# Three gate-column buffers and three one-hot buffers instead of two and four, with smaller kept tiles, in a decoder step on one core

## The chip, the cores and the metric

One core of one Trainium2 chip runs the whole program. The metric is the device time of one execution in microseconds (us); the median of three runs is shown, and beside it one execution under the hardware profiler. Engines are named as the profile names them: PE (TensorE, matrix products), DVE (VectorE), ACT (ScalarE), POOL (GpSimd, here only the issuer of row gathers) and SP (SyncE, here only the issuer of the other DMA transfers). Each engine works through its own queue in order, so an instruction that waits holds everything behind it on that engine.

## The reference, cut to what matters

The reference is one decoder layer for 512 prompt tokens and 64 sample tokens (576 rows of width 1024). Attention and a gating unit come first and give x1. The part that the change touches is the retrieval of single-neuron experts behind it:

```
sc = einsum('thcd,hcnd->thcn', q, sub_keys)             # 8 heads, 2 halves, 128 keys
s_top, i_top = top_k(sc, 16);  best, pos = top_k(sums of the two halves, 16)
idx = i*128 + j of the 16 best pairs                    # 16384 experts
gate = softmax(best)
w = gate * gelu(expert_u[idx] . x);  out[t] = sum_k w_k * expert_v[idx_k]
x2 = x1 + out;   x3 = x2 + sigmoid(rmsnorm(x2) @ w_ple_gate) * (p @ w_ple)
```

## The kernel before

The 576 columns are cut in two kinds. The 64 sample tokens and 128 of the prompt tokens are done by *gathering*: POOL fetches each token's expert rows from HBM by index (L726), and DVE makes the dot products (L737) and later the weighted sums (L744). The other 384 prompt tokens are done *densely*: for all 128 blocks of 128 experts, stage 1 computes gelu(u x) for all 384 tokens, the result is multiplied by a gate matrix G which is zero except at the retrieved experts, and stage 2 multiplies by v.

Stage 1 for one block j (function `stage1`, L781) loads 512 KB of weights by SP (L75), splits them on ACT into a rounded part `w_hi` (L70) and on DVE into the rest `w_lo` (L71), issues 24 PE products of 384 columns (L86) and one ACT gelu (L795). Results stay in SBUF, or are spilled to `ad` and fetched back.

G is built between about 572 and 817 us of the span by `build_g` (L856), called for `tb` = 0 to 23, 16 tokens each. It has four groups of four tokens. A group is: DVE writes the one-hot rows and columns `hot` (L870); ACT (L876, four instructions) or DVE (L879) scales one half by the gate into `og`; PE makes 8 small f16 products (L887) into a PSUM bank; ACT copies the bank into the gate-column tile `gs` (L891). After four groups one DMA writes the 1 MB of `gs` to `gd` in DRAM (L894), in runs of 512 bytes. `hot` and `og` come from the pool `op` with `OPB` = 4 buffers each; `gs` comes from two single pools in turn (L860, L916), so the first copy of block tb waits until the DMA of block tb-2 has landed. The build of G shares PE, ACT and DVE with stage 1, with the last top-k work of retrieval (up to `tb` = 7) and with gathers.

The order on each engine is fixed when the kernel is built, from the order of the program and from priorities given by hand: the splits of weights are drawn forward (L78, offset 1000), the products and copies of G too (L884, offset `RUNP` = 400), and `after` (L94) places an instruction behind another without a semaphore. How many gathers are issued between two steps is a budget (`pay`, L769). How many stage-1 blocks stand between two calls of `build_g` is a goal by arithmetic (L929 to L934).

Behind the last block the pools of the build are closed (L946), and their place is used by stage 2 (L947 to L949): `wh`, `wl`, `x1c` and two tiles `gs` of 12 KB per partition that bring G back. To spare the first of these a round trip, the columns of the last block go through a small tile `g0` (L928, written at L893, read at L1055).

Small tiles that live long: `ones` (128 x 128, L104) for sums over partitions at L158, L185 and L576; `eps` (three columns, L101); `dots`, `idx` and `gate` of the two gathered tiles (L734, L711, L695), each with two buffers of full width.

Of the kernel before, what the change touches and what calls it, by code (L numbers as in the profile page):

```python
# [7 lines left out]
F32 = mybir.dt.float32  # L8
# [3 lines left out]
U32 = mybir.dt.uint32  # L12
# [6 lines left out]
P = 128  # L19
# [5 lines left out]
NJ = 128  # L25
TB = 16
JB = 8
# [8 lines left out]
S1_TOPK = (4, 9, 13)  # L36
TBK = 7
S1_END = 6
OPB = 4
G_LAG = 3  # L40
RUNP = 400
RING = 44
# [9 lines left out]
def tile_decoder_step(ctx: ExitStack, tc: tile.TileContext, a, o):  # L52
    nc = tc.nc
    V, A, T, G, S = nc.vector, nc.scalar, nc.tensor, nc.gpsimd, nc.sync

    def pool(stack, name, bufs, side="left", **kw):
        return stack.enter_context(tc.tile_pool(name=name, bufs=bufs, side=side, reuse_waits="tile", **kw))

    const = pool(ctx, "const", 1)
# [34 lines left out]
    def after(ins, earlier):  # L94
        tc.add_manual_dep(ins.ins, earlier.ins.name, mybir.DependencyInfo(
            mybir.DependencyClass.NoSync, mybir.DependencyReason.DATA), reason="pace")
# [1 line left out]
    def mm():  # L98
        return psM.tile([P, 512], F32, name="mm")

    eps = const.tile([P, 3], F32, name="eps")  # L101
    V.memset(eps[:, 0:1], EPS)
    V.memset(eps[:, 1:2], 64.0 * EPS)
    ones = const.tile([P, P], F32, name="ones")  # L104
    V.memset(ones, 1.0)
    x1d = dr.tile([KC, P, NB], F32, name="x1d")
    x1r = dr.tile([NB // P, P, D], F32, name="x1r")
    pld = dr.tile([NT, D], F32, name="pld")
# [7 lines left out]
    c4 = pool(c4s, "c4", 7, "right")  # L116
    e1 = pool(e1s, "e1", 2, "right")
    e2 = pool(e2s, "e2", 2, "right")

    def f4(dt=F32):  # L120
        return c4.tile([P, 4, NT], dt, name="c4")
# [11 lines left out]
    def bank(tag):  # L133
        return psB.tile([P, 512], F32, name=tag)
# [19 lines left out]
    def rstd_cols(tot, rs):  # L154
        ps = bank("sc")
        for c0, r in TILES:
            for p0 in range(0, P, r):
                T.matmul(ps[p0:p0 + r, c0 // P:c0 // P + 1], lhsT=tot[:, c0:c0 + r], rhs=ones[:, 0:1],  # L158
                         start=True, stop=True)
        A.activation(rs, ps[:, 0:5], AF.Sqrt, scale=1.0 / D, bias=eps[:, 0:1])  # L160
        V.reciprocal(rs, rs)
# [10 lines left out]
    tot, add = sumsq()  # L172
# [9 lines left out]
    with tc.high_priority(offset=500):  # L182
        for cols in HALVES:
            ps = bank("sc")[:, :cols.stop - cols.start]
# [289 lines left out]
    for i in range(24):  # L474
        if i < 8:
            t, g = (svT, suT)[i // 4], i % 4
# [36 lines left out]
    gp = pool(ctx, "gp", 2)  # L513
# [8 lines left out]
    tot, add = sumsq()  # L522
# [43 lines left out]
    tq = pool(tqs, "tq", 2)  # L566
    tks = ExitStack()
    tk = pool(tks, "tk", 1, "right")
    rn2 = tq.tile([P, NB], F32, name="rn2", bufs=1)

    def norm_row():
        ps = bank("pt")[:, :NB]
        for b in range(3):
            dg = tq.tile([P, P], F32, name="dg")
            A.activation(dg, ident, AF.Copy, scale=rs2[:, b + 1:b + 2])
            T.matmul(ps[:, b * P:(b + 1) * P], lhsT=ones, rhs=dg, start=True, stop=True)  # L576
        A.activation(rn2, ps, AF.Copy)

    def norm_x(k):
# [38 lines left out]
    def retrieve(ti, idx_out):  # L618
        nh = TOPK[ti][1]
        n = nh * 16  # L620
        s0, s1 = top[ti][:, 0, :nh], top[ti][:, 1, :nh]

        def new(name, shape, dt=BF16, pl=tk, **kw):
            t = pl.tile([P, 8] + list(shape), dt, name=name, **kw)
            return t[:, :nh]
# [66 lines left out]
        V.tensor_tensor(bb.rearrange("p h k -> p (h k)"), pos.rearrange("p h k -> p (h k)"), stv, op=ALU.subtract)  # L692
        bbp = spread(bb)
        e0 = lookup("e0", ge, d0[:, :, None, :].to_broadcast([P, nh, 16, 16]), False, 1)
        gt = new("gate", [16], F32, gp if idx_out else tk, bufs=2)  # L695
        V.tensor_tensor(gt, best, best[:, :, 0:1].to_broadcast([P, nh, 16]), op=ALU.subtract)
        b_ = TOPK[ti][0]
        A.activation(gt, gt, AF.Exp, scale=rs2[:, b_:b_ + 1])
# [9 lines left out]
        if not idx_out:  # L708
            found[ti] = e0, e1, gtf
            return  # L710
        idx = gp.tile([P, P], U32, name="idx")  # L711
        V.scalar_tensor_tensor(idx[:, :n], e1, 128.0, e0, op0=ALU.mult, op1=ALU.add)
        ixs.append(idx)
        gts.append(gtf)
# [16 lines left out]

    def gather_steps():
        for ti, ns in ((0, NS), (1, P)):
            dots = gp.tile([P, P], F32, name="dots")  # L734
            for s in range(ns):
                row_ = gather_row(a["peer_u"], ixs[ti][:, s:s + 1])
                V.scalar_tensor_tensor(row_, row_, 1.0, xrs[ti], op0=ALU.mult, op1=ALU.mult,  # L737
                                       accum_out=dots[:, s:s + 1])
                yield
            A.activation(dots[:, :ns], dots[:, :ns], AF.Gelu_apprx_tanh)  # L740
            V.tensor_tensor(dots[:, :ns], dots[:, :ns], gts[ti][:, :ns], op=ALU.mult)
            for s in range(ns):
                row_ = gather_row(a["peer_v"], ixs[ti][:, s:s + 1])
                V.scalar_tensor_tensor(accs[ti], row_, dots[:, s:s + 1], accs[ti], op0=ALU.mult, op1=ALU.add)  # L744
                yield
# [69 lines left out]
    held_x = [xp.tile([P, 6, NB], F32, name="x4") for _ in range(NXP // 6)]  # L815
# [40 lines left out]
    def build_g(tb):  # L856
        ti, t0 = divmod(tb * TB, P)
        ij, gpk = ewT[ti]
        gate = gpk.rearrange("p t h -> p (t h)").bitcast(F32)
        gs = gsp[(tb + 1) % 2].tile([P, NJ, TB], F32, name="gs")  # L860
        for t4 in range(0, TB, 4):
            pt = psB.tile([P, 512], F32, name=("sc", "pt")[t4 // 4 % 2])
            hot = op.tile([P, 2, 2, P, 2], F16, name="hot")
            og = op.tile([P, 4, P], F32, name="og")
            u0 = (t0 + t4) // 2

            def wide(x):
                return x.rearrange("p u f t -> p (u f) t")[:, :, None, :].to_broadcast([P, 4, P, 2])

            V.tensor_tensor(hot.rearrange("p u f j t -> p (u f) j t"), iota[:, None].to_broadcast([P, 4, P, 2]),  # L870
                            wide(ij[:, u0:u0 + 2]), op=ALU.is_equal)
            grp = tb * TB // 4 + t4 // 4
            c = t0 + t4
            if grp % 4 < 3 if tb < TBK else grp % 3 < 2:
                for t in range(4):
                    last = A.activation(og[:, t, :], hot[:, t // 2, 1, :, t % 2], AF.Copy,  # L876
                                        scale=gate[:, c + t:c + t + 1])
            else:
                last = V.tensor_tensor(og.rearrange("p (u t) j -> p u t j", t=2),  # L879
                                       hot[:, :, 1].rearrange("p u j t -> p u t j"),  # L880
                                       gate[:, c:c + 4].rearrange("p (u t) -> p u t", t=2)[:, :, :, None]
                                       .to_broadcast([P, 2, 2, P]), op=ALU.mult)
            right = og.rearrange("p t j -> p (t j)").bitcast(F16).rearrange("p (t j h) -> p t j h", t=4, h=2)
            with tc.high_priority(offset=RUNP):  # L884
                for t in range(4):
                    for h in range(2):
                        g_last[tb] = T.matmul(pt[:, t * P:(t + 1) * P], lhsT=hot[:, t // 2, 0, :, t % 2],  # L887
                                              rhs=right[:, t, :, 1 - h], start=h == 0, stop=h == 1)
                        if t == h == 0:
                            after(g_last[tb], last)  # L890
                A.activation(gs[:, :, t4:t4 + 4], pt.rearrange("p (t j) -> p j t", t=4), AF.Copy, scale=1.0 / GS)  # L891
        if tb == NB // TB - 1:
            A.activation(g0, gs[:, 0:JB, :], AF.Copy)  # L893
        S.dma_start(gd[:, :, tb].rearrange("c p j t -> p c (j t)"), gs.rearrange("p (c j) t -> p c (j t)", j=JB))  # L894
# [18 lines left out]
    gs_s = ExitStack()  # L913
    ep = pool(gs_s, "ep", 2)
    op = pool(gs_s, "op", OPB)
    gsp = [pool(gs_s, "gsp%d" % i, 1) for i in range(2)]  # L916
    phase[0] = 1
    rest_t = [retrieve(ti, False) for ti in (3, 4)]
    for tb in range(NB // TB):
        if tb == TBK:  # L920
            for i, r_ in enumerate(rest_t):
                for _ in r_:
                    pass
                make_ew(*found[5 - len(rest_t) + i])
            tks.close()
            late = pool(aLs, "aL", 1, "right")
            acp.append(late.tile([P, RING - NXP, NB], F32, name="aL"))
            g0 = late.tile([P, JB, TB], F32, name="g0")  # L928
        if tb < TBK:  # L929
            goal = S1_TOPK[2] + (tb + 1) * (S1_PRE - S1_TOPK[2]) // TBK  # L930
        else:
            goal = S1_PRE + (tb - TBK + 1) * (NSP + RING - 1 - S1_END - S1_PRE) // (NB // TB - TBK)
        while len(acts) < goal:
            stage1()  # L934
        if tb == 0:
            make_ew(*found[2])
        build_g(tb)
        for _ in range(2):
            if rest_t and next(rest_t[0], 1) == 1:
                rest_t.pop(0)  # L940
                make_ew(*found[4 - len(rest_t)])
        pay(GT[tb >= TBK] if tb < 22 else 0)
# [6 lines left out]
    gsp = [pool(ds, "gsl%d" % i, 1) for i in range(2)]  # L949
# [270 lines left out]
```

## Time and profile before

| | |
|---|---|
| median of three runs | 1717.13 us (1714.81 to 1718.23) |
| the profiled execution, its own time | 1715.17 us |
| span of the profile, first to last instruction | 1713.3 us |
| PE busy in the span | 1680.2 us (98%) |
| DVE, ACT, POOL busy | 1406.5, 806.9, 536.2 us |
| bytes moved | 459.11 MB, mean 268 GB/s |
| DMA writes `gd<-gs` | 24 of 1 MB each |

The tile that a row writes stands left of the arrow and those that it reads right of it. A row of the waits says which engine and line stood still, what ended that, how many us in total, how often, and the longest. A row of the windows gives for one stretch the busy us of each engine with the count of instructions, the granted clock of PE as a share of full speed, the mean busy share of the DMA engines, and GB/s. In a timeline row the bracket holds the idle time ahead of the instruction and what ended it. The chain in order of time follows the work that ended last, with start and duration.

### The profile page before, as it was taken

The page shows a single profiled execution, that of the slowest core. Times are in us where ns is not written, and L with a number is a line of the kernel's source. Part 1 is how long each engine was busy: PE and PEld are TensorE (multiplying, and loading weights), DVE is VectorE, ACT ScalarE, POOL GpSimd, SP SyncE. Part 2 cuts the span into 40 slices and gives each one's busy share as a digit, 9 for nine tenths or more (in the row PEclk, how much of TensorE's full clock was granted, in tenths as well). Part 3 has the DMA queues.
Part 4 walks back from the last instruction along what each step waited for, and adds up shares of the span by engine and source line. Part 5 has one row for each costly group of instructions (what it writes and reads, how often), then busy time and mean ns, then how long its engine had stood idle before and what let it go on. Part 6 is the DMA issues. An engine that isn't in the chain of part 4 may idle for free.

```text
span 1713.3 us, 27406 instructions
## 1 busy us (share of the span) xinstructions
PE 1680.2 (98%) x10040; PEld 1518.4 (89%) x10040; DVE 1406.5 (82%) x2725; ACT 806.9 (47%) x1399; POOL 536.2 (31%) x390
## 2 busy tenths in 40 slices
PE   8999999999999999899999999999999999999998
PEld 7988999999988899888988888899999888888877
DVE  7365566569899999898688899989888898999983
ACT  6566452343355888777433333333333433333352
POOL 0000000000002112343144454455565665666600
PEclk9999999999999999999999999999999999999999
DMA  6311222433247789999999999999999899999952
GB/s 235 101 54 59 75 96 87 156 111 103 72 160 262 238 265 303 347 393 359 326 341 367 366 379 396 397 395 369 374 356 365 329 380 344 356 378 375 375 198 80
DMA packets 179479, 459.11 MB, mean 268 GB/s; under 512 B 15504, under 2 KB 78992, under 8 KB 177296
## 3 DMA queue, kind: packets, MB, share of 16 engines
q1 hardware_dynamic: 123760, 255.29, 42.2%
q0 software_dynamic: 55584, 202.07, 31.6%
q8 instruction: 79, 1.29, 0.3%
q14 instruction: 56, 0.46, 0.1%
HBM read 420.67 MB, written 37.36 MB: 267 GB/s over the span
## 4 chain that ended last, share of the span: by engine, by line
PE 86%; DVE 6%; DMA 4%; ACT 3%; issue 1%; SPq 0%; ACTq 0%; DVEq 0%
PE mm L86 40%; PE oacc L1022 31%; PE pv L86 4%; DMA gd<-gs 3%; PE oacc L983 2%; DVE w_lo L71 1%; PE sc L86 1%; PE pt L887 1%; ACT w_hi L70 1%; PE mm L983 1%; PE sc L887 1%; PE sc L596 1%; PE pv L338 1%; ACT og L876 0%; DMA w_raw<-peer_uT 0%
## 5 line engine op out<-in xcount | busy, mean ns | idle before, releaser
L726 POOL DMA_INDIRECT row<-peer_u,idx x192 | 262.8, 1369 | 812.5 <-PE pv L86 470.3
L70 ACT ACTIVATE w_hi<-w_raw 128x1024 fp32r<-128x1024 f32 x321 | 340.0, 1059 | 372.2 <-PE mm L86 279.4
L71 DVE TENSOR_TENSOR w_lo<-w_raw,w_hi 128x1024 fp32r<-128x1024 f32 x321 | 391.4, 1219 | 80.9 <-ACT w_hi L70 79.8
L86 PE MATMUL mm<-xd,w_hi 128*128 128x384 f32 x1552 | 401.6, 337 | 0.0
L726 POOL DMA_INDIRECT row<-peer_v,idx x192 | 272.0, 1417 | 237.8 <-DVE acc L744 159.2
L86 PE MATMUL mm<-x,w_hi 128*128 128x320 f32 (+1 forms) x1504 | 308.1, 299 | 0.0
L86 PEld LDWEIGHTS mm<-xd,w_hi 128*128 128x128 f32 x1552 | 282.0, 188 | 6.5
L86 PE MATMUL mm<-xd,w_lo 128*128 128x384 f32 x776 | 262.0, 338 | 0.0
L744 DVE SCALAR_TENSOR_TENSOR acc<-row,dots,acc 128x1024 f32<-128x1024 f32 x192 | 245.4, 1278 | 4.8 <-DMA row<-peer_v,idx 4.6
L86 PEld LDWEIGHTS mm<-x,w_hi 128*128 128x128 f32 x1504 | 241.8, 190 | 8.2 <-issue 7.4
L737 DVE SCALAR_TENSOR_TENSOR row<-row,xr 128x1024 f32<-128x1024 f32 x192 | 232.1, 1219 | 14.0 <-DMA row<-peer_u,idx 14.0
L1022 PE MATMUL oacc<-w_hi,wh 128*128 128x512 f32 x768 | 241.2, 394 | 0.0
L1022 PE MATMUL oacc<-w_hi,wl 128*128 128x512 f32 x768 | 241.0, 394 | 0.0
L1022 PE MATMUL oacc<-w_lo,wh 128*128 128x512 f32 x768 | 240.9, 394 | 0.0
L86 PE MATMUL mm<-x,w_lo 128*128 128x320 f32 (+1 forms) x752 | 223.1, 297 | 0.0
L1022 PEld LDWEIGHTS oacc<-w_hi,wl 128*128 128x128 f32 x768 | 143.6, 187 | 35.5
L1022 PEld LDWEIGHTS oacc<-w_lo,wh 128*128 128x128 f32 x768 | 143.6, 187 | 35.5
L1022 PEld LDWEIGHTS oacc<-w_hi,wh 128*128 128x128 f32 x768 | 143.0, 187 | 29.4
L86 PEld LDWEIGHTS mm<-xd,w_lo 128*128 128x128 f32 x776 | 146.0, 188 | 0.0
L86 PEld LDWEIGHTS mm<-x,w_lo 128*128 128x128 f32 x752 | 142.4, 189 | 1.0 <-issue 0.8
L86 PE MATMUL pv<-xd,w_hi 128*128 128x384 f32 x496 | 133.8, 345 | 0.0
L70 ACT ACTIVATE wh<-x 128x384 fp32r<-128x384 f32 x66 | 34.6, 525 | 166.0 <-PE oacc L1022 165.9
(331 smaller groups left out, 2119.7 us busy)
## 6 DMA issues: line engine op xcount, KB each, us to landing
w_raw<-peer_uT SPq DMA_DIRECT2D x128, 512.0 KB
w_raw<-peer_v SPq DMA_DIRECT2D x128, 512.0 KB
gd<-gs SPq DMA_DIRECT2D x24, 1024.0 KB
gs<-gd SPq DMA_DIRECT2D x15, 1536.0 KB
w_raw<-w_in SPq DMA_DIRECT2D x30, 512.0 KB
w_raw<-peer_wq SPq DMA_DIRECT2D x16, 512.0 KB
w_raw<-w_br SPq DMA_DIRECT2D x8, 512.0 KB
w_raw<-w_out SPq DMA_DIRECT2D x8, 512.0 KB
```

The source lines that it names most:

```text
L70: A.activation(hi, src, AF.Copy)
L71: V.tensor_sub(lo, src, hi.bitcast(F32))
L86: mark_pe[0] = T.matmul(ps, lhsT=w[wi][:, wk + k, :], rhs=x[xi][k], start=i == 0, stop=i == n - 1)
L338: ins = T.matmul(pvs[pr, :], lhsT=vt[:, t0 + j, pr], rhs=pT, start=j == 0, stop=j == nj - 1)
L596: T.matmul(ps[:, b * P:(b + 1) * P], lhsT=qp[:, b * P:(b + 1) * P], rhs=sk, start=True, stop=True)
L726: ins = G.indirect_dma_start(out=row_, out_offset=None, in_=table, in_offset=bass.IndirectOffsetOnAxis(ap=ix, axis=0))
L737: V.scalar_tensor_tensor(row_, row_, 1.0, xrs[ti], op0=ALU.mult, op1=ALU.mult, accum_out=dots[:, s:s + 1])
L744: V.scalar_tensor_tensor(accs[ti], row_, dots[:, s:s + 1], accs[ti], op0=ALU.mult, op1=ALU.add)
L887: g_last[tb] = T.matmul(pt[:, t * P:(t + 1) * P], lhsT=hot[:, t // 2, 0, :, t % 2], rhs=right[:, t, :, 1 - h], start=h == 0, stop=h == 1)
L983: T.matmul(p[:r, :hs.stop - hs.start], lhsT=xi[:, k, :r], rhs=w[k][wi][:, hs], start=k == 0 and xi is xh and wi == 0, stop=k == KC - 1 and ...
L1022: mark_pe[0] = T.matmul(oacc[t][hh], lhsT=wi[:, ts], rhs=vi[:, hh * 512:(hh + 1) * 512], start=j == 0 and last == 0 and vi is vh, stop=j = ...
```

## The change

The constant `OPB` goes from 4 to 3: three buffers each for `hot` and `og`. `gs` goes from two pools to three, used in the order `tb % 3`: the first copy of block tb then waits for the DMA of block tb-3. One `gs` tile is 8 KB per partition, one `hot` and one `og` are 2 KB each, so the three pools of the build take 38 KB instead of 34 KB.

The rest makes room. `ones` leaves the pool that lives for the whole run: it is put in the early pool `e2` for its first use, a second copy `ones_n` is written in the pool `tq` for `norm_row`, and the one-column sums of L158 read a new fourth column of `eps` instead. `dots`, `idx` and `gate` of the gathered tiles become one tile each of their own width. `g0` becomes a view of the sixth slot of the last held activation tile. No arithmetic changes.

```diff
-OPB = 4
+OPB = 3
...
-    eps = const.tile([P, 3], F32, name="eps")
+    eps = const.tile([P, 4], F32, name="eps")
...
-    ones = const.tile([P, P], F32, name="ones")
-    V.memset(ones, 1.0)
+    V.memset(eps[:, 3:4], 1.0)
...
+    ones = e2.tile([P, P], F32, name="ones", bufs=1)
+    V.memset(ones, 1.0)
...
-                T.matmul(ps[p0:p0 + r, c0 // P:c0 // P + 1], lhsT=tot[:, c0:c0 + r], rhs=ones[:, 0:1],
+                T.matmul(ps[p0:p0 + r, c0 // P:c0 // P + 1], lhsT=tot[:, c0:c0 + r], rhs=eps[:, 3:4],
...
+    ones_n = tq.tile([P, P], F32, name="ones", bufs=1)
+    V.memset(ones_n, 1.0)
...
-            T.matmul(ps[:, b * P:(b + 1) * P], lhsT=ones, rhs=dg, start=True, stop=True)
+            T.matmul(ps[:, b * P:(b + 1) * P], lhsT=ones_n, rhs=dg, start=True, stop=True)
...
-        gt = new("gate", [16], F32, gp if idx_out else tk, bufs=2)
+        if idx_out:
+            gt = gp.tile([P, nh, 16], F32, name="gate%d" % ti, bufs=1)
+        else:
+            gt = new("gate", [16], F32, bufs=2)
...
-        idx = gp.tile([P, P], U32, name="idx")
+        idx = gp.tile([P, n], U32, name="idx%d" % ti, bufs=1)
...
-            dots = gp.tile([P, P], F32, name="dots")
+            dots = gp.tile([P, ns], F32, name="dots%d" % ti, bufs=1)
...
-        gs = gsp[(tb + 1) % 2].tile([P, NJ, TB], F32, name="gs")
+        gs = gsp[tb % 3].tile([P, NJ, TB], F32, name="gs")
...
-    gsp = [pool(gs_s, "gsp%d" % i, 1) for i in range(2)]
+    gsp = [pool(gs_s, "gsp%d" % i, 1) for i in range(3)]
...
-            g0 = late.tile([P, JB, TB], F32, name="g0")
+            g0 = held_x[-1][:, 5, :JB * TB].rearrange("p (j t) -> p j t", j=JB)
```

## The prediction

> **What bounds the kernel now.** I began with the page: the busy shares and the chain that ended last.
>
> ```profile
> PE 1680.2 (98%) x10040; PEld 1518.4 (89%) x10040; DVE 1406.5 (82%) x2725; ACT 806.9 (47%) x1399; POOL 536.2 (31%) x390
> PE 86%; DVE 6%; DMA 4%; ACT 3%; issue 1%; SPq 0%; ACTq 0%; DVEq 0%
> ```
>
> PE is the engine that sets the end nearly everywhere, so a change gains only where PE stands still or runs slowly. The second look was at the windows, cut around the build of G (about 572 to 817 us) and over most of stage 2.
>
> ```profile
> core 0: us, PE busy (x) PEld busy (x) DVE busy (x) ACT busy (x) POOL busy (x), PEclk, DMA share, GB/s
> 572.00:640.00 68.00, 67.56 (x495) 62.70 (x494) 67.09 (x177) 61.28 (x134) 12.01 (x9) 1.00 0.82 258
> 640.00:693.00 53.00, 52.32 (x405) 48.70 (x404) 51.20 (x82) 44.36 (x101) 15.39 (x13) 1.00 0.93 311
> 693.00:708.00 15.00, 10.30 (x68) 9.37 (x65) 8.49 (x15) 7.72 (x17) 4.38 (x4) 0.77 1.02 339
> 708.00:747.00 39.00, 38.91 (x303) 36.53 (x301) 38.81 (x61) 31.96 (x77) 19.88 (x15) 1.00 1.04 361
> 747.00:754.00 7.00, 5.00 (x42) 4.16 (x41) 4.54 (x8) 4.05 (x11) 2.15 (x2) 1.00 1.06 395
> 754.00:800.00 46.00, 46.00 (x369) 42.77 (x368) 45.86 (x72) 39.55 (x97) 22.33 (x16) 1.00 1.07 391
> 800.00:817.00 17.00, 12.82 (x102) 11.29 (x102) 6.06 (x9) 10.79 (x29) 0.00 (x0) 0.90 0.88 289
> 817.00:838.00 21.00, 21.00 (x122) 20.86 (x122) 11.70 (x17) 9.11 (x15) 0.00 (x0) 1.00 0.90 321
> 838.00:1473.00 635.00, 635.00 (x3125) 563.74 (x3124) 565.59 (x734) 227.35 (x307) 341.36 (x245) 1.00 0.97 367
> 680.00:817.00 137.00, 126.04 (x976) 116.37 (x975) 116.75 (x179) 104.00 (x253) 55.10 (x41) 0.96 1.03 365
> ```
>
> Three short stretches stand out: 693 to 708, 747 to 754 and 800 to 817. Only there are PE and DVE both idle, and in two of them the clock is below 1.00. In the long stretches between them DVE is as full as PE (67.09 of 68.00, 38.81 of 39.00, 45.86 of 46.00): the build runs on two full engines. Stage 2 behind it has PE busy for all of 635 us. So what PE wins in the build arrives at the end of the program, and what DVE loses there does too.
>
> Who ends these idle times is in the waits between 640 and 817 us:
>
> ```profile
> ACT gs L891 <- DMA gd<-gs: 13.5, 5, 5.2
> PE pt L887 <- ACT og L876: 7.3, 4, 4.7
> PE sc L887 <- ACT og L876: 4.2, 4, 1.7
> DVE w_lo L71 <- ACT w_hi L70: 10.8, 5, 4.8
> DVE hot L870 <- PE sc L887: 2.8, 2, 2.5
> ```
>
> The first row is the root: ACT, about to copy into `gs`, waits for the write-out of the block two before. `og` and `w_hi` are queued behind that copy on ACT, and so PE (rows two and three) and DVE (row four) stop too. The chain in order of time has the same transfers as its longest pieces of this part, with start and duration:
>
> ```profile
> 660.05 8.56 DMA gd<-gs
> 685.61 13.07 DMA gd<-gs
> 735.81 14.47 DMA gd<-gs
> 798.59 10.50 DMA gd<-gs
> L894 SPq DMA_DIRECT2D gd<-gs x24: 370/377/616, 582.4 to 816.9; - x24
> ```
>
> The last row counts the write-outs: 24 from 582.4 to 816.9, one in 10.2 us. A write-out of 10 to 14.5 us does not fit in one block's time. The timeline shows the first stall, on ACT, DVE and PE:
>
> ```profile
> 698.78 0.60 ACT L891 ACTIVATE gs<-sc 128x512 f32<-128x512 f32 x1 [5.21 <-DMA gd<-gs]
> 700.36 1.23 DVE L71 TENSOR_TENSOR w_lo<-w_raw,w_hi 128x1024 fp32r<-128x1024 f32 x1 [4.79 <-ACT w_hi L70]
> 701.05 1.24 PE L887 MATMUL pt<-og,hot 128*128 128x128 f16 x8 [4.70 <-ACT og L876]
> 702.04 0.99 PE L86 MATMUL pv<-xd,w_hi 128*128 128x384 f32 x2
> 705.63 0.51 PE L86 MATMUL mm<-xd,w_hi 128*128 128x384 f32 x2
> ```
>
> PE stood 4.70 us and then ran at half pace (0.99 us for a pair that takes 0.51) until shortly before 705.63. The other two stalls begin the same way on ACT:
>
> ```profile
> 750.36 0.60 ACT L891 ACTIVATE gs<-sc 128x512 f32<-128x512 f32 x1 [2.95 <-DMA gd<-gs]
> 803.28 0.60 ACT L891 ACTIVATE gs<-sc 128x512 f32<-128x512 f32 x1 [2.58 <-DMA gd<-gs]
> 809.19 0.60 ACT L891 ACTIVATE gs<-sc 128x512 f32<-128x512 f32 x1 [2.24 <-DMA gd<-gs]
> ```
>
> **The third gate-column buffer.** The copy now waits for the block three before. That transfer has one more block's time, about 10 us, and the longest wait seen is 5.21, so I expect all five waits to go. What that gives PE: in the first stall 4.70 idle, and about 4.0 us at half pace (701.05 to just over 705), half of which, 2.0, is lost: 6.7. In the second 7.00 - 5.00 = 2.0. In the third 17.00 - 12.82 = 4.2 idle, and (1 - 0.90) x 17 = 1.7 of clock: 5.9. The sum is 14.6. Next late is DVE, since it is full elsewhere: it was idle 15.00 - 8.49 = 6.5 and 7.00 - 4.54 = 2.5 in the first two, so it allows 6.5 and 2.0. In the third little of DVE's work is left (6.06 of 17) and ACT's queue sets the pace; it gets back its two waits, 2.58 + 2.24 = 4.8. That makes 6.5 + 2.0 + 4.8 = 13.3.
>
> The bytes set a lower bound. From 680 to 817 us the core moved 365 GB/s x 137 us = 50.0 MB. At the 391 GB/s of the stretch in which PE had no idle time (754 to 800), these need 128 us, which allows 9 us; whether more than 391 can be had this trace does not show beyond the 395 of one short window. I take 12, between 9 and 13.3 and nearer to the end that follows from the three stalls, and keep 9 and 14.6 for the range.
>
> The Trainium skill speaks against this gain: "DMA: Bandwidth & Descriptors", section Specifications, gives about 358 GB/s as the limit of HBM for one core. By that the 50.0 MB need 140 us, and the third buffer would gain nothing. The trace does not agree: 391 GB/s over 46 us and 367 over 635 us are above it.
>
> **One one-hot buffer less.** `hot` (DVE) must now wait for PE's products of the third group before, not the fourth. With four buffers DVE waited 2.8 us at this place, of which the longest, 2.5, falls into the third stall; 0.3 is left. With three I look for places where `hot` was written before PE had read the third one back. The three longest outside the stalls, a DVE row and the PE row that it would wait for:
>
> ```profile
> 583.92 0.67 DVE L870 TENSOR_TENSOR hot<-iota,ij 128x1024 f16<-128x1024 f16 x1
> 585.94 0.64 PE L887 MATMUL pt<-og,hot 128*128 128x128 f16 x8
> 632.90 0.68 DVE L870 TENSOR_TENSOR hot<-iota,ij 128x1024 f16<-128x1024 f16 x1
> 635.66 0.72 PE L887 MATMUL pt<-og,hot 128*128 128x128 f16 x8
> 661.97 1.89 DVE L870 TENSOR_TENSOR hot<-iota,ij 128x1024 f16<-128x1024 f16 x3
> 665.16 0.67 PE L887 MATMUL sc<-og,hot 128*128 128x128 f16 x8
> ```
>
> These are 585.94 + 0.64 - 583.92 = 2.7, then 635.66 + 0.72 - 632.90 = 3.5, and for the last of the three in the fifth row (it starts about 663.2) 665.16 + 0.67 - 663.2 = 2.6; together 8.8 us. If the order on DVE stayed as it is, these would be waits, with `w_lo` of the next stage-1 block queued behind, and PE behind that. But the order is set at the build with the buffers known, and DVE has other work to put first: weight splits and gather products of 1.2 us. So the cost lies between 0.3 (what four buffers cost in that order) and 8.8 (the old order with three). I take 3, a third of the upper end, because DVE is full and has no spare time in which a wait would not count. ACT's `og` has three buffers as well; it is freed by the same products, so it waits at the same places and not in addition.
>
> **The small tiles.** The column sums and the memset of before:
>
> ```profile
> 356.14 1.26 PE L158 MATMUL sc<-ones,rstd 128*64 128x1 f32 x12
> L105 DVE MEMSET ones<- x1: 165/165/165, 0.9 to 0.9; 128x128 f32 x1
> L151 ACT ACTIVATE eps<-t x2: 203/203/203, 21.9 to 356.5; 128x1 f32<-128x1 f32 x2
> ```
>
> L158 now reads `eps`, into which ACT writes another column at 356.5 (L151). If the whole tile is taken as one, the sums starting at 356.14 wait until 356.7, 0.6 us of PE; if columns are told apart, nothing. The second memset costs DVE 0.165 us. A gain from either has no reason in the trace. I take 0.3 for both, from 0 to 0.8. The narrower `dots`, `idx` and `gate` issue the same instructions, at nothing: each was written once per gathered tile, so no wait on a shared buffer is taken away or added. `g0` in the held tile is written and read by the same two ACT copies; the slot's next writer is a gelu of stage 2, issued behind the read on the same engine, so no cover is needed. The pools of stage 2 shift against those of the build, but the first `gs` that comes back lies over the buffers of the last two blocks as before, and PE works without a break from 817 to 838 above it.
>
> **Sum.** -12 + 3 + 0.3 = -8.7. The profiled execution, 1715.17 (span 1713.3 and 1.9 around it), becomes 1706.5. The median of the runs shown, 1717.13, lies 2.0 above it; my figure is for a median: 1717.1 - 8.7 = 1708.4.
>
> **The rivals.** *The one-hots become the bound, and the kernel is slower.* Place: DVE's queue in blocks 0 to 23. Price: the mean of the three above, 2.9 us for each block that has one such wait. It decides from (12 + 3.4) / 2.9 = 5.3, so from six of 24 blocks on; with seven it is 20.3 - 12 + 0.3 = +8.6, some 1726. For it: DVE is at 99% between the stalls, and stage 1's weight splits stand in the same queue. Against it: only three of the leads are this long, and the order is made anew. Chance 0.16.
>
> *The one-hots eat the gain.* Three to five such blocks cost 9 to 14.5 against 12: 1714 to 1720, most of it no difference. Chance 0.13.
>
> *Transfers are the bound.* If 365 GB/s is all that this mix of 512-byte runs, weight loads and gathers gives, the stage keeps its 137 us; PE's stalls move from `gd<-gs` to the loading of weights, and the price of the one-hots comes on top: 1717 to 1720. For it: the DMA share is at 1.02 to 1.07 from 693 to 800. Against it: 46 us at 391 GB/s without a gap of PE. Chance 0.05. By the 358 GB/s of the Trainium skill, "DMA: Bandwidth & Descriptors", section Specifications, it would be the likeliest.
>
> *The waits do not go*, because a write-out that may take longer does so. It would need over 20 us from issue to landing where 14.47 is the longest in the chain. That leaves DVE's 3 us: 1720. Chance 0.02.
>
> **How the numbers follow.** The forecast has 0.64: from 1717.1 - 14.6 + 0.3 = 1702.8 to 1717.1 - 9 + 5 = 1713 (the least gain, and 5 for the one-hots). What a measurement can tell from no change is 0.2%, 3.4 us. Faster: the forecast and a small part of the second rival, 0.65. Slower by over 3.4: the first rival and the upper edge of the others, 0.18. The same: 0.17. The range goes from 1701 (the lower end, less the 2 us by which single runs of before lie off their median) to 1722, which leaves out most of the first rival and little else.
>
> **What would show it.** Right: no wait of `gs` on `gd<-gs` in the build; PE's clock at 1.00 from 572 to 817; the build some 9 us shorter, and everything behind it moved by that; above 370 GB/s from 680 on. The one-hot term shows in the waits of L870 on PE, and in DVE's idle time ahead of `hot`. Wrong: `hot` waiting over 12 us in total, new idle time of PE ahead of `w_lo` products, or waits of L70 on weight loads.

## The result and the profile after

The kernel after the change takes 1702.76 us (median of 4 runs, 1701.00 to 1703.32) against 1716.41 us of the kernel before (4 runs, 1714.81 to 1718.23). The ratio is 0.9921, with a 95% interval of 0.9905 to 0.9936: 13.6 us less, where 8.7 less was predicted. Ratios here and below leave out a single execution, one with three `og` that took 2323.85 us at a clock of 0.655. The profiled execution took 1701.0 us with a span of 1699.2, against 1715.17 and 1713.3. The change moves line numbers by six in the build: `hot` is L876, `og` L882 and L885, the products L893, the copy into `gs` L897, the write-out L900, and stage 2's products are L1028.

The busy shares and the chain's shares by engine, from the page of the kernel after:

```profile
PE 1676.4 (99%) x10040; PEld 1515.9 (89%) x10040; DVE 1405.4 (83%) x2727; ACT 806.8 (47%) x1399; POOL 543.0 (32%) x390
PE 88%; DVE 7%; ACT 2%; DMA 1%; issue 1%; SPq 0%; ACTq 0%; DVEq 0%
```

The engines do nearly the same work (PE 1676.4 us, 1680.2 before), and transfers are 1% of the chain instead of 4%. Where the time went is seen from three rows of each kernel: the first and last start of `hot`, of the products of G, and of the products of stage 2. The products of G go to two PSUM banks in turn, and the row is that of the bank that was written last (`sc` before, `pt` after). First the kernel before, then the kernel after:

```profile
L870 DVE TENSOR_TENSOR hot<-iota,ij x96: 632/682/760, 573.4 to 806.4; 128x1024 f16<-128x1024 f16 x96
L887 PE MATMUL sc<-og,hot x384: 217/218/330, 575.5 to 816.0; 128*128 128x128 f16 x192
L1022 PE MATMUL oacc<-w_hi,wh x768: 394/394/502, 837.3 to 1650.3; 128*128 128x512 f32 x192
```

```profile
L876 DVE TENSOR_TENSOR hot<-iota,ij x96: 670/683/734, 572.0 to 798.8; 128x1024 f16<-128x1024 f16 x96
L893 PE MATMUL pt<-og,hot x384: 217/218/312, 576.3 to 804.3; 128*128 128x128 f16 x192
L1028 PE MATMUL oacc<-w_hi,wh x768: 394/394/502, 823.2 to 1636.2; 128*128 128x512 f32 x192
```

From the first `hot` to the last product of G there were 816.0 - 573.4 = 242.6 us, and now 804.3 - 572.0 = 232.3: 10.3 less. From there to the first product of stage 2, in which PE does what still stands of stage 1 ahead of it, there were 837.3 - 816.0 = 21.3 us, and now 823.2 - 804.3 = 18.9: 2.4 less. Stage 2 takes 813.0 us in both (837.3 to 1650.3, 823.2 to 1636.2), so what the build wins arrives at the end in full. The remaining 1.4 lies ahead of the first `hot`; in a second profile of the changed kernel that start lies at 569.6 instead of 572.0, so 1.4 is within the scatter of single executions.

The windows of the kernel after, over the build and its end:

```profile
core 0: us, PE busy (x) PEld busy (x) DVE busy (x) ACT busy (x) POOL busy (x), PEclk, DMA share, GB/s
572.00:640.00 68.00, 67.15 (x495) 62.58 (x494) 66.46 (x175) 61.08 (x132) 12.94 (x10) 1.00 0.79 255
640.00:693.00 53.00, 53.00 (x399) 49.80 (x398) 51.99 (x83) 42.84 (x95) 18.24 (x14) 1.00 0.93 317
693.00:747.00 54.00, 53.91 (x435) 49.62 (x434) 53.39 (x83) 47.24 (x116) 27.66 (x20) 1.00 1.07 392
747.00:800.00 53.00, 51.15 (x410) 47.24 (x408) 48.41 (x73) 44.65 (x110) 22.25 (x16) 0.97 1.06 380
800.00:817.00 17.00, 17.00 (x115) 16.69 (x114) 3.60 (x4) 8.21 (x18) 0.00 (x0) 1.00 1.06 328
```

The stretches of 693 to 708, 747 to 754 and 800 to 817, in which PE stood before, are full. One short stop is left, within 747 to 800 (51.15 of 53.00), and there the clock is 0.97 on the mean. The waits of the kernel after between 572 and 826:

```profile
DVE w_lo L71 <- ACT w_hi L70: 16.3, 4, 7.6
ACT gs L1061 <- DMA gd<-gs: 7.2, 1, 7.2
...
ACT gs L897 <- DMA gd<-gs: 2.4, 2, 2.1
DVE hot L876 <- PE pt L893: 2.3, 3, 1.4
...
DVE hot L876 <- PE sc L893: 0.2, 1, 0.2
```

The wait of the copy on the write-out fell from 13.5 us to 2.4. The 7.2 us of L1061 are at 815, behind the build; PE has work of stage 1 above it (17.00 of 17.00).

The one wait that is left can be followed through two engines. ACT's timeline of the kernel after, the last copy of block 19 and the first of block 22:

```profile
771.14 0.60 ACT L897 ACTIVATE gs<-pt 128x512 f32<-128x512 f32 x1
...
792.78 0.60 ACT L897 ACTIVATE gs<-sc 128x512 f32<-128x512 f32 x1 [2.14 <-DMA gd<-gs]
```

SP's timeline, where "SPq" rows are the issuing of transfers:

```profile
770.03 7.65 SPq L75 DMA_DIRECT2D w_raw<-peer_uT  x2
778.10 0.38 SPq L900 DMA_DIRECT2D gd<-gs  x1
778.58 9.35 SPq L75 DMA_DIRECT2D w_raw<-peer_uT  x1
787.98 0.47 SPq L900 DMA_DIRECT2D gd<-gs  x1
```

And the chain in order of time has the transfer:

```profile
778.10 14.60 DMA gd<-gs
```

Block 19 was complete at 771.14 + 0.60 = 771.7, but SP was in the middle of issuing two weight loads that wait for their buffers, and issued the write-out at 778.1, 6.4 us late. It landed at 778.10 + 14.60 = 792.7, and the copy that needs its buffer started at 792.78. PE stood 1.84 us behind it. In the kernel before, no write-out but one left more than 0.4 us after its last copy, so this lateness came with the change.

### The profile page after: what moved, and what is told of

Its sections match the earlier page's. It is cut to its first block, busy times and chain, and to the rows that moved or that the text cites. A ratio compares the mean times of both kernels' runs of the same rounds, so it can differ in the third digit from the quotient of the medians.

```text
span 1699.2 us, 27435 instructions
## 1 busy us (share of the span) xinstructions
PE 1676.4 (99%) x10040; PEld 1515.9 (89%) x10040; DVE 1405.4 (83%) x2727; ACT 806.8 (47%) x1399; POOL 543.0 (32%) x390
## 4 chain that ended last, share of the span: by engine, by line
PE 88%; DVE 7%; ACT 2%; DMA 1%; issue 1%; SPq 0%; ACTq 0%; DVEq 0%
PE mm L86 41%; PE oacc L1028 32%; PE pv L86 5%; PE oacc L989 2%; DVE w_lo L71 2%; PE sc L86 2%; PE sc L893 1%; PE pt L893 1%; DMA gd<-gs 1%; PE mm L989 1%; PE sc L599 1%; ACT w_hi L70 1%; PE pv L339 1%; PE pv L843 0%; DVE row L743 0%
## 5 line engine op out<-in xcount | busy, mean ns | idle before, releaser
L70 ACT ACTIVATE w_hi<-w_raw 128x1024 fp32r<-128x1024 f32 x321 | 339.9, 1059 | 362.2 <-PE mm L86 260.4
L732 POOL DMA_INDIRECT row<-peer_v,idx x192 | 276.2, 1438 | 228.5 <-DVE acc L750 154.5
L1028 PE MATMUL oacc<-w_hi,wh 128*128 128x512 f32 x768 | 241.2, 394 | 0.0
L1028 PE MATMUL oacc<-w_hi,wl 128*128 128x512 f32 x768 | 241.0, 394 | 0.0
L1028 PE MATMUL oacc<-w_lo,wh 128*128 128x512 f32 x768 | 240.9, 394 | 0.0
L1028 PEld LDWEIGHTS oacc<-w_hi,wl 128*128 128x128 f32 x768 | 143.6, 187 | 35.5
L1028 PEld LDWEIGHTS oacc<-w_lo,wh 128*128 128x128 f32 x768 | 143.6, 187 | 35.4
L1028 PEld LDWEIGHTS oacc<-w_hi,wh 128*128 128x128 f32 x768 | 143.0, 187 | 29.5
L70 ACT ACTIVATE wh<-x 128x384 fp32r<-128x384 f32 x66 | 34.6, 525 | 169.5 <-PE oacc L1028 163.2
```

The lines of the kernel that those rows point to most:

```text
L70: A.activation(hi, src, AF.Copy)
L732: ins = G.indirect_dma_start(out=row_, out_offset=None, in_=table, in_offset=bass.IndirectOffsetOnAxis(ap=ix, axis=0))
L1028: mark_pe[0] = T.matmul(oacc[t][hh], lhsT=wi[:, ts], rhs=vi[:, hh * 512:(hh + 1) * 512], start=j == 0 and last == 0 and vi is vh, stop=j = ...
```

## Experiments

After the result my theory was that of the prediction: the third gate-column buffer gives about 12 us and the missing one-hot buffer costs a little. The rival was that part of the gain comes from the one-hots. Ratios are to runs of the kernel before on the same chip, with 95% intervals; one thousandth is 1.7 us.

**Three one-hots alone.** Two `gs` as before:

```diff
-OPB = 4
+OPB = 3
```

> Only the one-hots go from four buffers to three; the gate columns keep two. Theory A (the third gate-column buffer gives all of the gain, and one one-hot buffer less costs nothing, because the order on DVE is made anew for three): within 2 us of before. Theory B (as predicted: the one-hots cost about 3 us, hidden behind a larger gain of the gate columns): 3 us slower than before, at most 8.8. If the waits of hot on PE grow, they show in the trace outside the three stalls.

Measured: 1711.99 us, ratio 0.9970 (0.9956 to 0.9985), some 5 us faster. The term that was predicted as a cost is a gain. The waits of `hot` on PE are there (6.2 us over the build, 2.6 and 3.6 by bank), and the kernel is faster all the same.

**The small tiles alone.** All of the change except `OPB` and the third pool of `gs`:

> Everything of the change but the two buffer counts: small tiles made smaller or moved, two gate-column buffers, four one-hots. Theories A and B: no difference, within 1.5 us of before, with the same five waits of gs on its write-out. Theory C (part of the gain comes from where the tiles now lie: 1.1 us at the head of the program and 2.4 us behind the last gate-column block were seen in the profile of the change): 1 to 3.5 us faster than before.

Measured: 1716.06 us, ratio 0.9992 (0.9975 to 1.0008): no difference that can be told. By the interval a gain of up to 4 us is not excluded; all the rest is in the two buffer counts.

**Three gate columns with two one-hots, and the change once more.** The first is the kernel after with one line changed:

```diff
-OPB = 3
+OPB = 2
```

> The change with two one-hot buffers instead of three. Theory A: the price of a one-hot buffer is small down to two, at most 3 us over the change, so still some 10 us faster than before. Theory B: one buffer less costs at least what the step from four to three did, 3 us or more, and it grows, since with two buffers DVE can be only one group ahead of PE: 6 us or more over the change, so at most 8 us faster than before.

> The change itself, beside the three others on the same chip: 0.9921 of before, between 0.9905 and 0.9936, by the measurement on record; about 13.6 us faster.

Measured: 1706.94 us, ratio 0.9940 (0.9918 to 0.9963), and for the change 1701.82 us, ratio 0.9910 (0.9888 to 0.9933). With two one-hots most of the gain is still there, but 5 us of it are gone by the medians (1705.32 to 1708.80 in six runs, against 1698.88 to 1703.40 in six of the change). Three is better than two and, by the first experiment, with two gate columns, better than four.

**Four one-hots beside three gate columns.** The room for them is taken from the gathered rows; to keep the comparison clean, both kernels have it taken away:

```diff
-    rowp = pool(rows, "rowp", 5)
+    rowp = pool(rows, "rowp", 4)
```

and the second has `OPB = 4` too.

> The change with four row buffers for the gathers instead of five; this makes 4 KB of room and is the partner of the next run. The gathers' buffer has no price by either theory as long as DVE finds its rows: 1702 to 1706, that is 12 to 16 us faster than before; if gathers come late, slower than the change by what DVE waits for rows.

> The same with four one-hot buffers: three gate-column buffers and four one-hots, which does not fit beside five row buffers. Against its partner it gives the price of the fourth one-hot where no gate-column wait is left. As predicted (a one-hot less costs 3): 3 us faster than the partner. By the first run of this study (with two gate-column buffers, three one-hots were 5 us faster than four): if the smaller number spreads the groups and helps by itself, 2 to 5 us slower than the partner; if it only made the waits on write-outs shorter, the two are equal within 1.5 us.

Measured: 1742.16 us, ratio 1.0168 (1.0146 to 1.0191), and 1744.20 us, ratio 1.0164 (1.0139 to 1.0188). The fifth row buffer is worth some 40 us against the change, and that hides in the time what the one-hots do: nothing follows from these two times for the one-hots. Over the same stretch of stage 2, first the kernel after, then the one with four rows and three one-hots:

```profile
838.00:1460.00 622.00, 622.00 (x3059) 552.03 (x3059) 558.12 (x725) 222.31 (x300) 341.68 (x243) 1.00 0.98 369
```

```profile
838.00:1460.00 622.00, 609.03 (x2974) 536.98 (x2972) 539.54 (x706) 216.54 (x292) 331.85 (x235) 0.99 0.96 359
```

PE, which did not stop at all there, stops 13 us. The whole of stage 2 takes 847.1 us instead of 813.0 (824.7 to 1671.8). The waits of the second kernel between 838 and 1500 say for what; the first of these rows was 11.9 us in 13 times in the kernel after:

```profile
DVE row L743 <- DMA row<-peer_u,idx: 49.8, 44, 5.0
...
PE mm L86 <- DVE w_lo L71: 8.5, 4, 5.3
```

DVE waits for gathered rows, and the weight splits behind it in its queue come late to PE.

The build lies ahead of that, and it can be read in these two profiles, in which DVE waits for rows 5.5 and 7.7 us from 560 to 850 us. The waits of the copy on the write-out, first with three one-hots, then with four:

```profile
ACT gs L897 <- DMA gd<-gs: 0.2, 1, 0.2
```

```profile
ACT gs L897 <- DMA gd<-gs: 0.7, 1, 0.7
```

So the third gate column takes these waits away beside four one-hots too, 13.5 us down to 0.7. From the first `hot` to the first product of stage 2, PE does the same products of stage 1 and of G in all kernels of this table, whose entries are single executions:

| us from the first `hot` to stage 2 | four `hot` | three `hot` |
|---|---|---|
| two `gs`, five row buffers | 263.9 (before), 266.1 (small tiles alone), 273.5 (three `og`, below) | 260.5 (three of both), 261.5 (three `hot` alone, below) |
| three `gs`, four row buffers | 257.5 (571.2 to 828.7) | 253.0 (571.7 to 824.7) |
| three `gs`, five row buffers | not built, no room | 251.2 and 250.3 (the change), 253.2 (the last experiment) |

With four `hot` the third gate column is worth 6.4 us or more in this stretch, with three 7.3 or more, and three `hot` are better than four in both rows.

**The write-out issued by ACT.** In the kernel after, SP issues write-outs late, as shown above. Here ACT issues them:

```diff
-        S.dma_start(gd[:, :, tb].rearrange("c p j t -> p c (j t)"), gs.rearrange("p (c j) t -> p c (j t)", j=JB))
+        A.dma_start(gd[:, :, tb].rearrange("c p j t -> p c (j t)"), gs.rearrange("p (c j) t -> p c (j t)", j=JB))
```

> The change with the write-out of the gate columns issued by ACT, right behind its last copy, instead of by SP, where it stood up to 8.3 us behind weight loads that wait for a free buffer. If that lateness is what still makes one gs copy wait 2.1 to 2.5 us in the change, that wait goes: 2 to 4 us faster than the change (its idle time of 1.8 to 2.3 and up to 1.7 of clock). If the issue itself, 24 times about 0.4 us on ACT, counts, it gives that back: no difference. Rival: weight loads then come earlier and compete, no gain.

Measured: 1745.10 us, ratio 1.0160 (1.0139 to 1.0181), some 43 us more than the change where 2 to 4 less or no difference was expected. No wait of `gs` on a write-out is left in the build, but the order on ACT, DVE and PE came out quite different with the instruction in ACT's queue. Its waits:

```profile
DVE w_lo L71 <- ACT w_hi L70: 50.5, 26, 5.2
ACT w_hi L70 <- PE mm L86: 36.1, 17, 3.0
...
ACT w_hi L70 <- PE pv L86: 28.2, 12, 4.2
```

Stage 1's own splits and products now wait for each other (26 waits of `w_lo` against 4). What the lateness alone costs cannot be read from this kernel.

**The write-out done twice.** The kernel after with a second copy of every block sent to a scratch tensor that nothing reads; it adds 24 transfers of 1 MB:

```diff
+    gd2 = dr.tile([NJ // JB, P, NB // TB, JB, TB], F32, name="gd2")
...
+        S.dma_start(gd2[:, :, tb].rearrange("c p j t -> p c (j t)"), gs.rearrange("p (c j) t -> p c (j t)", j=JB))
```

> The change with every write-out made twice, the second into a scratch tensor that nobody reads: 24 MB more in the build, about a third more than it moves. If transfers have room (the rival of the prediction falls): the third buffer still hides most of it, at most 8 us slower than the change, so faster than before. If the DMA engines are the bound: 24 MB at 391 GB/s are 64 us, and most of them show: 30 us or more slower than the change.

Measured: 1778.96 us, ratio 1.0364 (1.0343 to 1.0384), 77 us more than the change. Its windows over the build:

```profile
680.00:720.00 40.00, 27.78 (x188) 25.94 (x186) 24.45 (x38) 19.82 (x48) 11.07 (x10) 0.83 1.03 336
720.00:760.00 40.00, 26.42 (x194) 24.10 (x194) 22.70 (x35) 20.96 (x52) 9.36 (x8) 0.82 1.09 353
760.00:800.00 40.00, 31.22 (x215) 28.85 (x214) 28.24 (x45) 22.73 (x56) 13.70 (x11) 0.84 1.07 355
```

The DMA share is 1.03 to 1.09, as in the kernel after, and PE stands for a fifth to a third of the time. In its waits from 572 to 880 us there is one that the kernel after does not have, ACT's on weight loads:

```profile
ACT w_hi L70 <- DMA w_raw<-peer_uT: 46.8, 11, 9.7
```

24 MB at about 350 GB/s take some 70 us, nearly all of the 77. So transfers bound the build of this kernel, and the kernel after, at the same DMA share from 693 us on, should be near to that bound; how near was not measured. The order on PE, DVE, ACT and SP is another one here too; what part of the 77 us it has was not measured.

**Which of the two one-hot tiles it is.** The kernel before with three `hot` and four `og`, then with four `hot` and three `og`; two `gs` in both:

```diff
-            hot = op.tile([P, 2, 2, P, 2], F16, name="hot")
+            hot = op.tile([P, 2, 2, P, 2], F16, name="hot", bufs=3)
```

```diff
-            og = op.tile([P, 4, P], F32, name="og")
+            og = op.tile([P, 4, P], F32, name="og", bufs=3)
```

> The kernel before with three buffers for hot and four for og; gs keeps two, small tiles as before. Three of both, with two gs, measured 0.997 of the kernel before (some 5 us less), and in that profile stage 1 had 4.5 blocks left behind the last G product instead of 5.0. Theory H (the gain comes from hot: with three of them DVE's gather products run less far ahead, and its weight splits for stage 1 come earlier): 1709 to 1713, ratio 0.996 to 0.998, and 4.5 blocks left. Theory O (it comes from og, the copies of ACT): no difference, 1715 to 1718, and 5.0 blocks left.

> The kernel before with four buffers for hot and three for og; gs keeps two, small tiles as before. Theory H (hot counts): no difference, 1715 to 1718. Theory O (og counts: ACT's 0.26 us copies wait, and the copies of weights, w_hi, come ahead of them): 1709 to 1713, ratio 0.996 to 0.998. If both this and the other one come out between, the two act together.

Measured: 1712.04 us, ratio 0.9967 (0.9953 to 0.9982), and 1719.45 us, ratio 1.0008 (0.9988 to 1.0029). The whole gain of the one-hots is that of `hot`; `og` gives none that can be told. (A copy into `og` took 0.39 us on the median in the kernel before, not the 0.26 of this expectation.) First three `hot`, then three `og`, in the rows that were shown of before:

```profile
L870 DVE TENSOR_TENSOR hot<-iota,ij x96: 673/685/741, 572.6 to 806.0; 128x1024 f16<-128x1024 f16 x96
L887 PE MATMUL pt<-og,hot x384: 217/218/312, 576.9 to 815.2; 128*128 128x128 f16 x192
L1022 PE MATMUL oacc<-w_hi,wh x768: 394/394/502, 834.1 to 1647.1; 128*128 128x512 f32 x192
```

```profile
L870 DVE TENSOR_TENSOR hot<-iota,ij x96: 631/684/706, 571.5 to 813.0; 128x1024 f16<-128x1024 f16 x96
L887 PE MATMUL sc<-og,hot x384: 217/219/330, 573.6 to 823.7; 128*128 128x128 f16 x192
L1022 PE MATMUL oacc<-w_hi,wh x768: 393/394/503, 845.0 to 1658.0; 128*128 128x512 f32 x192
```

With three `hot` the build is as long as before (815.2 - 572.6 = 242.6), but only 834.1 - 815.2 = 18.9 us of stage 1 are left between it and stage 2, as in the kernel after; with four they are 845.0 - 823.7 = 21.3, as before. The order, which is made when the kernel is built, is another. From the first `hot` to the last copy into `gs`, PE, DVE, ACT and SP each have the same instructions in the same order in the kernel before, with the small tiles alone, with three `og`, and with four one-hots beside three gate columns; and one other order, again the same on all four engines (but for the last issue of SP in one of them), in the kernel after, with three `hot`, with three of both, and in the kernel with four row buffers and three one-hots. Among these the count of `hot` alone chooses between the two. The third `gs` changes nothing in the order. How the two orders differ can be counted: the products of stage 1 that PE has between the first G products of neighbouring blocks, from block 8 to block 23:

```
four hot:   29 60 15 63 27 24 69 27 38 33 43 31 42 27 18
three hot:  48 41 45 34 27 38 33 43 31 42 27 39 33 31 16
```

With four, these blocks of G come in bursts (15, then 63 products apart); with three they are spread more evenly. Ahead of block 8 it is the other way round (at most 78 apart with four, 118 with three), but no wait of 0.5 us or more on a write-out falls there. With three, 14 products of stage 1 fewer stand behind the start of the last group (1692 against 1706, counted to the end of the program): PE has done them within a build of the same length. A write-out takes 8.6 to 14.5 us in the chain of before, however its block came, so that evenly spaced blocks should run less deep into it; this link is argued. Windows and waits, first before, then three `hot`:

```profile
640.00:817.00 177.00, 165.36 (x1277) 152.82 (x1276) 154.94 (x240) 138.43 (x328) 64.14 (x49) 0.97 1.00 347
```

```profile
640.00:817.00 177.00, 168.20 (x1291) 154.99 (x1291) 156.88 (x240) 140.51 (x331) 67.14 (x48) 0.98 1.00 349
```

```profile
ACT gs L891 <- DMA gd<-gs: 11.0, 6, 3.0
...
PE pt L887 <- ACT og L876: 5.8, 6, 2.5
```

PE stands 11.6 us in that stretch before and 8.8 with three `hot`, at a slightly better clock. The longest wait of the copy is 3.0 us instead of 5.2, and PE's longest behind it 2.5 instead of 4.7: the waits become shorter pieces. In the kernel with three of both, which has the same order, these two are 3.9 and 3.7 us, so that the size varies from one execution to the next. The order and this gain belong together in these runs; a kernel with four `hot` in the order of three was not tried, so that the order is the cause is likely but not shown by itself. Shorter waits on write-outs seem not to be all of it: beside three `gs`, where these waits are 0.7 and 0.2 us, the order with three still came to stage 2 4.5 us earlier in the table above (one execution each).

**Five one-hots.** The kernel before with the small tiles, which make the room, and `OPB = 5`:

> The kernel before with the small tiles of the change (alone they measured 0.9992) and five buffers each for hot and og instead of four; two gs. Theory T (a trend: the fewer one-hots, the less of G runs ahead of stage 1, and the better): slower than before by 2 to 5 us, ratio 1.001 to 1.003, with 5.5 blocks of stage 1 left behind the last G product and a wait of gs on its write-out above 13 us. Theory N (no trend, three happens to give a better order): within 2 us of before, ratio 0.999 to 1.001.

Measured: 1718.84 us, ratio 1.0008 (0.9992 to 1.0024): no difference that can be told. What stays behind the last product of G follows the count (818.7 to 841.2, 22.5 us; 21.3 with four, 18.9 with three, and 18.4 with two beside three `gs`), but the time does not follow it from four to five. So it is no rule that fewer are better; the order with three is a better one. Both the kernel with five and the one with two have orders of their own.

**The write-out called for earlier.** The kernel after with the write-out at a higher priority:

```diff
+        with tc.high_priority(offset=RUNP):
-        S.dma_start(gd[:, :, tb].rearrange("c p j t -> p c (j t)"), gs.rearrange("p (c j) t -> p c (j t)", j=JB))
+            S.dma_start(gd[:, :, tb].rearrange("c p j t -> p c (j t)"), gs.rearrange("p (c j) t -> p c (j t)", j=JB))
```

> The kernel after with the write-out of gs given to the planner of the order as due 400 instructions earlier, so that SP issues it ahead of the weight loads that wait for their buffers; same queue, same bytes. In the kernel after, write-outs were issued 50.5 us late in the sum over 24 blocks, 8.3 us at most, and one wait of gs of 2.1 to 2.5 us is left. Theory L (lateness costs that wait and the half pace of PE behind it): the sum of lateness falls below 10 us, no gs wait is left in the build, 1699 to 1702, ratio to before 0.990 or a little less. Rival (the weight loads that are pushed behind the write-out come later and cost as much, or the order of the other engines changes with it): same as the kernel after or slower, 1702 to 1710, with waits of w_hi on w_raw in place of the gs wait.

Measured: 1702.00 us, ratio 0.9907 (0.9882 to 0.9932), the same as the change. The edit did not do what it was meant to do: the order on SP and on every other engine is that of the kernel after, and 2.5 us of waits of `gs` are left. It is a third measurement of the change (0.9921, 0.9910, 0.9907), and what the late issue costs stays open.

## Why the prediction was right, and where it failed

**The number.** 1702.76 us lies within the range from 1701 to 1722, at the lower end of the stretch from 1702.8 to 1713 that the forecast named. In part that is luck: the gate columns gave 2.2 us less than was taken and the one-hots 8 us more, and the two errors are of opposite sign.

**The bound.** Right. PE's stops in the build were the place, everything behind it moved by what the build and its tail won, and stage 2 kept its 813 us.

**The third gate-column buffer, 12 us between 9 and 14.6.** Right, and measured nearly by itself, since the kernel with three `hot` and two `gs` and the kernel after have the same order: 0.9967 against 0.9910, a difference of 0.0057 or 9.8 us, with some 4.5 us of uncertainty from the two intervals. Three of both against the change, on one chip, give 1711.99 - 1701.82 = 10.2 us. From 640 to 817 us, PE's idle time falls from 177 - 168.20 = 8.8 to 1.95 us by this row of the kernel after, and the clock goes from 0.98 to 0.99:

```profile
640.00:817.00 177.00, 175.05 (x1351) 163.35 (x1350) 157.38 (x241) 142.94 (x336) 68.16 (x48) 0.99 1.02 360
```

That is 6.9 of idle time and about 1.8 of clock, 8.7 together. In the old order the third buffer has larger stalls to remove, 11.6 us of idle time instead of 8.8, but it was not measured there by its time: four one-hots beside three gate columns take the room of a gather row. The profile without that row shows the waits gone (0.7 us) and stage 2 reached 6.4 us earlier than in the profile of before.

The step "I expect all five waits to go" was nearly right: 13.5 us became 2.4. What it left out is that the write-out does not start when the block is complete. SP issued the one of block 19 6.4 us late, behind loads that waited for DVE. The prediction gave the transfer "one more block's time, about 10 us", and SP's queue took more than half of that. The rival that the waits do not go asked for over 20 us from issue to landing; for block 19 it was 14.60 from issue, but 21.0 from its last copy (771.7 to 792.7).

**One one-hot buffer less, +3 between 0.3 and 8.8.** This is the step that failed, by its sign: -5 us where +3 was taken (0.9970 with three of both, 0.9967 with three `hot`). The waits themselves lie in the range: 2.3 + 0.2 = 2.5 us of `hot` on PE in the kernel after, 6.2 with three of both. (Its upper end was drawn from the three longest leads of before alone; all leads outside the third stall add up to some 17 us.) But they were priced in the old order, while the sentence that the order is made anew at the build was used only to make the cost smaller. A new order can be better as well as worse, and the range of this term should have reached below nothing. With -5 and -9.8, and the 0.3 of the small tiles as predicted, the sum is -14.5 against the measured -13.6; this is no check, since the -9.8 was got as what is left of the whole.

**The small tiles, +0.3 between 0 and 0.8.** Nothing speaks against it: 0.9992 (0.9975 to 1.0008), an interval wider than the term. The sums on the new column of `eps` did not wait for ACT's write to it; their row in the kernel after has no idle time but 0.2 us for `rstd`:

```profile
L159 PE MATMUL sc<-eps,rstd x12: 197/250/271, 355.0 to 356.0; 128*128 128x1 f32 x8, 128*64 128x1 f32 x4
```

**The rivals.** That one-hots become the bound, or eat the gain, is wrong: three of both alone are faster, and their waits stayed small. That transfers are the bound at 365 GB/s is wrong, since the kernel after moves 392 GB/s for 54 us. The Trainium skill, "HBM Reference", section "Specifications (TRN2)", gives about 358 GB/s as the share of one core, but adds that a core that streams alone measures well above it, some 425 GB/s; the 392 GB/s lie between the two figures, above the share, and the prediction weighed only the first. Still the transfers are near: with the write-out sent twice they bound the build at the same DMA share, so that they may well limit what a further buffer could win. That the waits do not go is wrong too, but for the 2.4 us.

**The signs that were named.** The build 9 us shorter: 10.3, and 2.4 in the tail. Above 370 GB/s from 680 on: 392 and 380 up to 800. The clock at 1.00 from 572 to 817: no, 0.97 from 747 to 800, from one stop of 1.84 us. New idle time of PE ahead of `w_lo` products: none. `hot` waiting over 12 us: 2.5. Waits of L70 on weight loads: none in the build.

## What to carry to other kernels

Changing a buffer count in a kernel whose order is fixed at its build changes two things, the waits and the order, and the second can be larger and of either sign: compare the order of the instructions before a wait is priced in the old one. A buffer behind a transfer needs the time from the data being complete to the landing, and the issuing queue is a part of it: here a write-out behind loads that waited for buffers left 6.4 us late. When a change has several parts, measure them alone; here the smallest edit, one digit, brought some 5 of 13.6 us, and its sign was wrong on paper.

## What the runs showed of the hardware

The clock fell after a very short stop, and not each time. In the kernel after, PE stood 1.84 us ahead of 795.15. These windows are cut where the clock changes; each is 3.41 us long:

```profile
792.81:796.22 3.41, 1.56 (x14) 1.16 (x12) 1.86 (x3) 3.41 (x8) 0.00 (x0) 1.00 1.07 366
796.22:799.63 3.41, 3.41 (x23) 3.26 (x22) 1.86 (x3) 2.73 (x8) 0.00 (x0) 0.50 1.07 331
799.63:803.05 3.42, 3.42 (x26) 3.26 (x25) 1.14 (x2) 3.06 (x8) 0.00 (x0) 1.00 1.08 336
```

In a second profile of the same kernel a stop of 2.25 us at the same place was followed by full clock. Its windows are cut in the same steps, counted back from a change of its clock at 1696.88:

```profile
788.93:792.35 3.42, 1.86 (x14) 1.58 (x13) 0.65 (x2) 1.68 (x3) 0.00 (x0) 1.00 1.02 355
792.35:795.76 3.41, 2.71 (x27) 2.40 (x27) 2.73 (x4) 3.41 (x11) 0.00 (x0) 1.00 1.12 337
795.76:799.17 3.41, 3.41 (x26) 3.15 (x25) 1.43 (x3) 3.31 (x8) 0.00 (x0) 1.00 1.03 328
```

The loss in the first is (1 - 0.50) x 3.41 = 1.7 us, one step at half pace. The stop of the first lies in one step, in which PE is idle for 3.41 - 1.56 = 1.85 us; the longer stop of the second is cut by the end of a step into 3.42 - 1.86 = 1.56 and 3.41 - 2.71 = 0.70 us. The Trainium skill, "TensorE: Matmul & The Clock Gate", section "Part 1: The HAM clock gate (the 'warmup' mystery)", describes a free-running window of 3.4 us, so that the same program can meet it differently from run to run; length and scatter agree with it. That a whole idle window is needed does not agree: the stop that was followed by half pace filled little more than half of one. All 14 traces, behind 480 us, give no sharp line: their clock falls to half 51 times, each time behind a step with 0.92 us of PE's idle time or more, all but once 1.45 or more, while the most idle step with full clock behind it has 1.94. The price of a stop of some 2 us was thus its length plus 0 or 1.7 us; behind the 4.70 us of the kernel before, about 4 us ran at half pace.

One row buffer of five for the gathers is worth 40 us in this kernel, about three times the change that was studied. It was not expected that the gathers, whose issuing engine is busy for 32% of the span, stand that near to the bound.
